# A Strassen–Winograd feed-forward block: seven products in one fixed PSUM tile, sums kept per product, four of them put back

## The chip, the cores and the metric

The kernel runs on one core of a Trainium2 chip. The metric is the device time of one execution in microseconds (us); lower is better. Engines: PE is the matrix engine (PEld its weight loads), DVE the vector engine, ACT the scalar engine, POOL the GpSimd engine, SP the engine that issues most DMAs. PSUM is the memory that PE writes; the other engines read it from there.

## The reference

One decoder layer for 544 tokens (512 of a prompt, 8 times 4 of samples): attention and gated delta rule, then cross attention, then a gated feed-forward block. The change touches only the last:

```python
    hf = rmsnorm(x, p['norm_ffn_g'])
    gate, up = jnp.split(hf @ p['w_gate_up'], 2, axis=-1)   # 2048 -> 2 x 5632
    x = x + (jax.nn.silu(gate) * up) @ p['w_down']          # 5632 -> 2048
```

All is float32.

## The kernel before, in words

Tokens lie side by side, T = 544 columns, in two halves of HT = 272; features lie on the 128 partitions. Every float32 operand is split exactly into two parts (a rounded high part by an ACT cast, the rest by a subtraction), and a product is three matmuls: high by high, high by low, low by high. Blocks of two by two are multiplied with Winograd's seven products P1 to P7 instead of eight.

**Gate and up** (`ffn`, the loop over `j`, 44 *rounds*). A round makes two output blocks of 128 features (one of gate, one of up) in `wino`: four *steps* `u`, each over two pairs of input blocks, each 42 matmuls of 272 columns (7 products x 2 pairs x 3). So a round has 168 matmuls, and a product is added up in PSUM over the four steps.

`left` makes a step's left operands: two DMAs of weights into `u`, four sums on POOL (L1613 to L1616), two casts on ACT (`wh`, 128x768 and 128x1024, L1620) and two subtractions on DVE (`wl`, L1621). `wh` and `wl` have two buffers each, so the casts of a step can begin when the step two before it has left PE. `combine` reads the seven products out of PSUM (ACT copies P1, L1661; DVE adds the others, L1673 to L1679), and `ffn` scales, applies silu and multiplies. Every second round POOL makes Winograd's four sums of the result (`sums`, L1572 to L1575) and ACT's queue stores them to `hT` in DRAM.

**Down** (the loop over `ci`, five *chunks* of 4, 4, 4, 4 and 6 pairs of hidden blocks). Each chunk has eight rounds `m` over the output blocks, of two steps (three in the last chunk). `fetch` loads a chunk's right operands from `hT` and splits them (L1590, L1591). After each round `combine` adds the two result blocks to `acc` (L1661 to L1671). The last chunk adds the residual `x` and stores.

**PSUM.** The products lie in two tiles of two banks out of a pool of two such tiles each (`c.mm`), and three single banks of four (`c.aux`).

**Order.** A scheduler of the language puts every engine's instructions in the order in which the program is written, with priorities; each engine then runs its own list strictly in order and waits on semaphores. The waits come from which tile an instruction reads or writes.

## Time and profile before

| | |
|---|---|
| median of 3 runs | 3056.04 us (3052.62 to 3064.1) |
| the profiled execution | span 3059.9 us; no other time of it is shown |
| granted PE clock, mean | 0.983 |
| PE, DVE, POOL, ACT busy | 95%, 70%, 55%, 45% of the span |
| gate and up | 1549.7 to 2491.9 us of the span |
| down | 2491.9 to 3059.9 us |
| DMA | 392.67 MB, mean 128 GB/s |

How to read it: times in the rows are microseconds, or nanoseconds for the mean of one instruction. In a timeline row the bracket at the end is the idle time of the engine just before, and the instruction that ended it. PEclk is the clock that PE was granted, as a part of full speed. Matmuls overlap: one shows about 0.29 us but the next starts 0.125 us later.

### The profile page before, as it was taken

The numbers are of one execution on the slowest core, as the hardware profiler recorded it, in microseconds if no ns is written. First come the engines' busy times: TensorE is split into PE (matmuls) and PEld (weight loads), VectorE is DVE, ScalarE is ACT, GpSimd is POOL, SyncE is SP. The second block draws the span as 40 slices with busy tenths as digits, with TensorE's granted clock in tenths as the row PEclk, the third lists the DMA queues.
The fourth block names the chain that finished last, engine by engine and source line by source line (L and its number), as shares of the span: only waits on it lengthen the run. The fifth ranks groups of instructions, "written<-read, shape, count | busy, mean of one in ns | idle before, by whom it ended". The sixth has DMA issues, their size and how long they took to land.

```text
span 3059.9 us, 58347 instructions
## 1 busy us (share of the span) xinstructions
PE 2900.2 (95%) x22118; PEld 2789.1 (91%) x22118; DVE 2134.3 (70%) x3339; ACT 1363.5 (45%) x2600; POOL 1671.8 (55%) x1784
## 2 busy tenths in 40 slices
PE   8999999999999999999799999999999989988898
PEld 7999998889899999999689999999999989988797
DVE  6776775655655655366687777777777888888865
ACT  5544453435645654245543343333333344334333
POOL 3211122312112100032378988898888977999997
PEclk9999999999999999999899999999999999999999
DMA  7323233544535765423434344333434354344343
GB/s 212 95 80 85 75 88 99 144 137 147 173 105 151 227 197 150 127 81 116 161 117 127 118 122 123 121 117 118 125 118 123 116 179 132 110 131 127 119 137 105
DMA packets 619505, 392.67 MB, mean 128 GB/s; under 512 B 36475, under 2 KB 572360, under 8 KB 619224
## 3 DMA queue, kind: packets, MB, share of 16 engines
q1 hardware_dynamic: 596904, 355.95, 39.6%
q10 hardware_dynamic: 22320, 32.99, 3.0%
q8 instruction: 174, 2.85, 0.4%
q14 instruction: 107, 0.88, 0.1%
HBM read 334.17 MB, written 54.68 MB: 127 GB/s over the span
## 4 chain that ended last, share of the span: by engine, by line
POOL 27%; PE 20%; DVE 8%; issue 4%; DMA 4%; ACT 2%; SPq 0%; POOLq 0%; ACTq 0%; DVEq 0%
PE mm L208 7%; POOL u L1615 6%; POOL u L1613 6%; POOL u L1614 5%; PE mm L1647 5%; POOL u L1616 5%; PE aux L1647 4%; DVE wl L1621 3%; DMA u<-in_w_gate_up 2%; DVE pr L1591 2%; PE aux L1342 2%; POOL acc L1670 1%; PE mm L1530 1%; POOL x L1572 1%; PE aux L960 1%
## 5 line engine op out<-in xcount | busy, mean ns | idle before, releaser
L1621 DVE TENSOR_TENSOR wl<-u,wh 128x768 fp32r<-128x768 f32 (+1 forms) x528 | 752.5, 1442 | 315.9 <-ACT wh L1620 213.6
L1647 PE MATMUL mm<-pr,wh 128*128 128x272 f32 x4224 | 830.6, 292 | 41.6 <-DVE acc L1663 25.3
L1620 ACT CAST wh<-u 128x768 fp32r<-128x768 f32 (+1 forms) x528 | 488.8, 943 | 826.5 <-PE aux L1647 295.4
L1647 PEld LDWEIGHTS mm<-pr,wh 128*128 128x128 f32 x4224 | 669.4, 191 | 50.5 <-DVE acc L1663 20.3
L1647 PE MATMUL aux<-pr,wh 128*128 128x272 f32 x3168 | 626.9, 292 | 17.7 <-DVE acc L1669 6.7
L1647 PE MATMUL mm<-pr,wl 128*128 128x272 f32 x2112 | 615.7, 292 | 22.5 <-DVE wl L1621 22.5
L208 PE MATMUL mm<-ah,wh 128*128 128x272 f32 (+1 forms) x2464 | 538.6, 298 | 5.7 <-ACT ah L321 4.6
L1647 PEld LDWEIGHTS aux<-pr,wh 128*128 128x128 f32 x3168 | 506.8, 192 | 21.7 <-DVE acc L1669 8.6
L208 PE MATMUL mm<-al,wh 128*128 128x272 f32 (+1 forms) x2464 | 524.3, 291 | 0.7 <-DVE al L239 0.7
L208 PE MATMUL mm<-ah,wl 128*128 128x272 f32 (+1 forms) x2464 | 515.6, 290 | 0.1
L1647 PE MATMUL aux<-pr,wl 128*128 128x272 f32 x1584 | 460.9, 291 | 2.0 <-DVE wl L1621 2.0
L1647 PEld LDWEIGHTS mm<-pr,wl 128*128 128x128 f32 x2112 | 403.3, 191 | 28.4 <-DVE wl L1621 28.4
L208 PEld LDWEIGHTS mm<-ah,wh 128*128 128x128 f32 (+1 forms) x2464 | 391.9, 189 | 28.8 <-issue 8.5
L197 DVE TENSOR_TENSOR wl<-wr,wh 128x512 fp32r<-128x512 f32 (+1 forms) x366 | 264.0, 725 | 195.9 <-ACT wh L196 186.7
L208 PEld LDWEIGHTS mm<-al,wh 128*128 128x128 f32 (+1 forms) x2464 | 389.6, 188 | 5.4 <-issue 2.0
L208 PEld LDWEIGHTS mm<-ah,wl 128*128 128x128 f32 (+1 forms) x2464 | 386.2, 188 | 2.5 <-DVE wl L197 0.5
L196 ACT CAST wh<-wr 128x512 fp32r<-128x512 f32 (+1 forms) x366 | 224.3, 615 | 336.6 <-PE mm L208 272.6
L1613 POOL TENSOR_TENSOR u<-u 128x256 f32<-128x256 f32 x264 | 277.3, 1050 | 140.8 <-DMA u<-in_w_gate_up 90.2
L1615 POOL TENSOR_TENSOR u<-u 128x256 f32<-128x256 f32 x264 | 323.2, 1224 | 0.0
L1616 POOL TENSOR_TENSOR u<-u 128x256 f32<-128x256 f32 x264 | 308.5, 1169 | 19.1
L1647 PEld LDWEIGHTS aux<-pr,wl 128*128 128x128 f32 x1584 | 303.7, 192 | 2.6 <-DVE wl L1621 2.4
L1614 POOL TENSOR_TENSOR u<-u 128x256 f32<-128x256 f32 x264 | 270.4, 1024 | 0.0
(518 smaller groups left out, 3809.1 us busy)
## 6 DMA issues: line engine op xcount, KB each, us to landing
u<-in_w_gate_up SPq DMA_DIRECT2D x352, 256.0 KB
wr<-in_w_in SPq DMA_DIRECT2D x108, 512.0 KB
u<-in_w_down SPq DMA_DIRECT2D x176, 256.0 KB
v<-hT SPq DMA_DIRECT2D x66, 272.0 KB
page<-in_cache_sb_k SPq DMA_DIRECT2D x128, 128.0 KB
page<-in_cache_sb_v SPq DMA_DIRECT2D x64, 256.0 KB
wr<-in_w_out SPq DMA_DIRECT2D x32, 512.0 KB
hT<-x ACTq DMA_DIRECT2D x44, 272.0 KB
```

The costliest lines, as they stand in the source:

```text
L196: nc.scalar.copy(hi[:, :m, :n], raw[:, k : k + m, :n])
L197: nc.vector.tensor_sub(lo[:, :m, :n], raw[:, k : k + m, :n], hi[:, :m, :n].bitcast(F32))
L208: c.nc.tensor.matmul(ps[:n, h, :HT], l[:, :n], r[:, h * HT : (h + 1) * HT], start=first and i == 0, stop=last and i == 2,)
L1342: nc.tensor.matmul(ps[:, :256], l, r, start=k == 0 and n == 0, stop=k == 7 and n == 2)
L1591: nc.vector.tensor_sub(lo[:, o : o + n * HT], x[:, : n * HT], hi[:, : n * HT].bitcast(F32))
L1613: nc.gpsimd.tensor_add(s1, a21, a22)
L1614: nc.gpsimd.tensor_sub(s3, a11, a21)
L1615: nc.gpsimd.tensor_sub(s2, s1, a11)
L1616: nc.gpsimd.tensor_sub(s4, a12, s2)
L1620: nc.scalar.copy(hi, u[:, o : o + n])
L1621: nc.vector.tensor_sub(lo, u[:, o : o + n], hi.bitcast(F32))
L1647: nc.tensor.matmul(ps, l[:, cols], r, start=u + i == 0 and j == 0, stop=u + i == n - 1 and j == 2)
```

## The change

What lies ahead of the feed-forward block is as it was. In it:

1. One PSUM tile `bank` of seven banks holds the seven products, in fixed places, for all rounds; `aux` has one bank left. Products are made in another order (P1, P7, P6, P2, P5, P4, P3).
2. `combine` is one ACT copy of P1 and five DVE operations (two of 544 columns), all on `bank`.
3. `left` puts the weights in `raw` and the sums in a tile of their own; three of the four sums go from POOL to DVE, with other formulas.
4. `hT` holds the split parts, seven tiles of 544 columns a pair. The split (ACT cast, POOL subtraction) is done once, in the gate-and-up loop, and seven stores a pair go out on ACT's queue. `fetch` is seven DMAs a pair on POOL's queue straight into the operand tiles.
5. In the down part, each of the eight rounds `m` keeps its seven product sums in SBUF (class `Sums`). P1, P6 and P7 are added to by DVE after each round; P2 to P5 are copied by ACT back into their banks ahead of the next chunk's round (`seed`), whose matmuls add to them, and are copied out by ACT after it. The residual is added in chunk 1. The combination is done once, in the last chunk (`finish`).

The core of the diff:

```diff
 def left(c, w, k, ca, cb):
-    u = c.wu.tile([P, 8, 2 * P], F32, tag="u", name="u", bufs=3)
+    a, b = (c.wu.tile([P, 4, 2 * P], F32, tag=x, name=x, bufs=n) for x, n in (("raw", 3), ("sum", 2)))
...
-    nc.gpsimd.tensor_add(s1, a21, a22)
-    nc.gpsimd.tensor_sub(s3, a11, a21)
-    nc.gpsimd.tensor_sub(s2, s1, a11)
-    nc.gpsimd.tensor_sub(s4, a12, s2)
+    nc.vector.tensor_sub(b[:, 2], a[:, 0], a[:, 2])
+    nc.vector.tensor_add(b[:, 1], b[:, 2], a[:, 1])
+    nc.gpsimd.tensor_add(b[:, 0], a[:, 0], a[:, 1])
+    nc.vector.tensor_sub(b[:, 3], a[:, 3], b[:, 1])
...
-    ma, mb = c.mm(), c.mm()
-    p4, p7, p3 = (c.aux()[:, :HT] for _ in range(3))
-    todo = ((p1, 1, 0), (p2, 2, 1), (p4, 0, 6), (p6, 4, 4), (p5, 3, 3), (p7, 5, 5), (p3, 6, 2))
+PRODUCTS = ((P1, 1, 0), (P7, 5, 5), (P6, 4, 4), (P2, 2, 1), (P5, 3, 3), (P4, 0, 6), (P3, 6, 2))
...
+                    nc.tensor.matmul(
+                        c.bank[:, p, :HT], l[:, cols], r,
+                        start=u + i == 0 and j == 0 and p not in seeded, stop=u + i == n - 1 and j == 2,
+                        skip_group_check=p in seeded,
+                    )
...
+def combine(c, y, z):
+    nc.scalar.copy(s1, bank[:, P1])
+    nc.vector.tensor_add(u2, s1, bank[:, P6])
+    nc.vector.tensor_add(y[:, :HT], s1, bank[:, P2])
+    nc.vector.tensor_add(halves(e), bc(u2.rearrange("p (o x) -> p o x", o=1), [P, 2, HT]), bank[:, P7 : P5 - 1 : -1])
+    nc.vector.tensor_add(halves(z), bc(u3.rearrange("p (o x) -> p o x", o=1), [P, 2, HT]), bank[:, P4 : P5 + 1])
+    nc.vector.tensor_add(y[:, HT:], u4, bank[:, P3])
...
+class Sums:
+    def seed(self):
+        for x, b, n in self.parts[3:1:-1]:
+            self.c.nc.scalar.copy(self.c.bank[:, b : b + n, :HT], x)
+    def keep(self, added=False):
+        for i, (x, b, n) in enumerate(self.parts):
+            if added and i < 2:
+                self.c.nc.vector.tensor_add(x, x, self.c.bank[:, b : b + n, :HT])
+            else:
+                self.c.nc.scalar.copy(x, self.c.bank[:, b : b + n, :HT])
...
+                nc.gpsimd.dma_start(t, src[:, i])
...
+            for i, x in enumerate((*v, *sums(c, *v, nc.gpsimd))):
+                hi, lo, n, _ = part_of(c, x, lambda: c.hp.tile([P, T], F32R, tag="st", name="hs", bufs=4), 2 if i else 1, nc.gpsimd)
+                for t in (hi, lo)[2 - n :]:
+                    nc.scalar.dma_start(hT[j // 2, :, len(tiles)], t[:, :].bitcast(F32))
...
+            wino(c, c.w_down, 2 * first[ci], m * P, (m + 1) * P, pairs, step, 0, SEEDED if ci else ())
+            acc[m // 2].keep(ci > 0)
+            if ci == 1:
+                acc[m // 2].residual(*x)
             if last:
+                acc[m // 2].finish()
...
+    c.bank = banks.tile([P, 7, 512], F32, name="bank")
+    c.aux = lambda: banks.tile([P, 512], F32, tag="aux", name="aux", bufs=1)
```

How the instructions stand now is shown at three places. In the rows, `waits PE_49` and the like name the engines whose semaphores an instruction waits on.

ACT at the end of a gate-and-up round (the twelfth), before: the copy of P1 out of PSUM is the row `COPY g<-mm`; the two casts ahead of it belong to the next round's first step, those behind it to its second and third.

```order
L1620 CAST wh<-u 128x768 [waits DMAHW5_49,DVE_49,DMAHW7_49,PE_49,Activation_49]
L1620 CAST wh<-u 128x1024 [waits DVE_49,PE_49,Pool_49]
L1661 COPY g<-mm 128x272 [waits PE_49]
L1620 CAST wh<-u 128x768 [waits DMAHW0_49,DMAHW1_49,DVE_49,PE_49]
L1620 CAST wh<-u 128x1024 [waits DVE_49,PE_49,Pool_49]
```

The same place after; `b` is the copy of P1, and the four casts are those of the next round's steps 0 and 1:

```order
L1624 CAST wh<-raw 128x768 [waits DMAHW0_49,DMAHW7_49,DVE_49,PE_49]
L1624 CAST wh<-sum 128x1024 [waits DVE_49,PE_49,Pool_49]
L1624 CAST wh<-raw 128x768 [waits DMAHW2_49,DMAHW3_49,DVE_49,PE_49]
L1624 CAST wh<-sum 128x1024 [waits DVE_49,PE_49,Pool_49]
L1668 COPY b<-bank 128x272 [waits PE_49]
L1749 ACTIVATE g<-g 128x544 [waits DVE_49]
L1594 CAST hs<-u 128x544 [waits DVE_49]
L1758 DMA hT<-hs 128x544 [waits Activation_49]
L1758 DMA hT<-hs 128x544 [waits Pool_49]
```

The copy of P1 moved from behind two casts of the next round to behind four, and its wait is now for the last matmul of the round, the last to write `bank`. Behind it, four split casts and seven stores take the place of three stores.

DVE at the same boundary, before; `b`, `g` and `u` are the combination's tiles:

```order
L1621 TENSOR_TENSOR wl<-u,wh 128x768 [waits DMAHW0_49,DMAHW1_49,PE_49,Activation_49]
L1673 TENSOR_TENSOR b<-g,mm 128x272 [waits PE_49]
L1674 TENSOR_TENSOR g<-g,mm 128x272 [waits DVE_49]
L1675 TENSOR_TENSOR g<-b,mm 128x272
L1676 TENSOR_TENSOR b<-b,aux 128x272 [waits PE_49]
L1679 TENSOR_TENSOR g<-g,aux 128x272 [waits DVE_49,PE_49]
L1677 TENSOR_TENSOR u<-b,mm 128x272 [waits DVE_49]
L1678 TENSOR_TENSOR u<-b,aux 128x272
```

And after:

```order
L1625 TENSOR_TENSOR wl<-raw,wh 128x768 [waits PE_49,Activation_49]
L1625 TENSOR_TENSOR wl<-sum,wh 128x1024 [waits PE_49,Activation_49]
L1669 TENSOR_TENSOR b<-b,bank 128x272 [waits Activation_49]
L1670 TENSOR_TENSOR g<-b,bank 128x272
L1671 TENSOR_TENSOR e<-b,bank 128x544 [waits DVE_49]
L1617 TENSOR_TENSOR sum<-raw 128x256 [waits DMAHW7_49,DMAHW6_49]
L1672 TENSOR_TENSOR u<-e,bank 128x544 [waits DVE_49]
L1673 TENSOR_TENSOR g<-e,bank 128x272
```

The `wl` of 1024 columns (of step 1) now stands ahead of the combination, and one weight sum (L1617) inside it.

PE at the start of a round, after (the first two rows are the last of the old round, P3):

```order
L1653 MATMUL bank<-pr,wh 128x272 x2
L1653 MATMUL bank<-pr,wl 128x272
L1653 MATMUL bank<-pr,wh 128x272 [waits DVE_49,Activation_49]
L1653 MATMUL bank<-pr,wh 128x272
L1653 MATMUL bank<-pr,wl 128x272
```

The round's first matmul (P1) waits there, in the program's semaphores, for the DVE row L1673 and the ACT row L1668 above; no later product's first matmul waits for a reader of its bank.

ACT at a round's end in the down part, before (chunk 1); `a` is P1's copy, `pr<-v` casts of fetched operands:

```order
L1590 CAST pr<-v 128x544 [waits DMAHW7_49]
L1590 CAST pr<-v 128x544 [waits DMAHW4_49]
L1620 CAST wh<-u 128x1024 [waits DVE_49,PE_49,Pool_49]
L1661 COPY a<-mm 128x272 [waits PE_49]
L1620 CAST wh<-u 128x768 [waits DMAHW6_49,DMAHW7_49,DVE_49,PE_49]
```

And after; `a_30334` and `a_30333` are the kept P4, P5 and P2, P3 of the round that ends, `a_30457` and `a_30458` those of the next round:

```order
L1624 CAST wh<-raw 128x768 [waits DMAHW6_49,DMAHW7_49,DVE_49,PE_49]
L1624 CAST wh<-sum 128x1024 [waits DVE_49,PE_49,Pool_49]
L1699 COPY a_30334<-bank 128x544 [waits DVE_49,PE_49,Activation_49]
L1699 COPY a_30333<-bank 128x544
L1691 COPY bank<-a_30457 128x2x272 [waits Activation_49]
L1691 COPY bank<-a_30458 128x2x272 [waits Activation_49]
L1624 CAST wh<-raw 128x768 [waits DMAHW1_49,DMAHW0_49,PE_49]
```

One copy of 272 columns became two copies out and two copies back, of 544 columns each.

## The prediction

> **What bounds the kernel now.** First the page's busy times and its slices, then stretches of the feed-forward part, then PE's timeline at the ends of rounds.

> ```profile
> PE 2900.2 (95%) x22118; PEld 2789.1 (91%) x22118; DVE 2134.3 (70%) x3339; ACT 1363.5 (45%) x2600; POOL 1671.8 (55%) x1784
> ...
> PEclk9999999999999999999899999999999999999999
> ```

> PE is busy 95% of the span at nearly full clock: the end is set by how rarely PE stands still. The change leaves all before 1549.7 us as it was, so I read the two parts behind it (columns: window, its length, then busy time of PE, PEld, DVE, ACT and POOL, granted clock, DMA share, GB/s).

> ```profile
> 1549.70:2491.90 942.20, 916.63 (x7229) 908.72 (x7229) 729.89 (x794) 366.96 (x448) 838.53 (x777) 1.00 0.41 124
> 1718.00:1761.30 43.30, 42.50 (x336) 42.18 (x336) 33.52 (x37) 16.76 (x21) 39.20 (x37) 1.00 0.39 120
> 2491.90:3059.90 568.00, 505.86 (x3773) 493.20 (x3773) 447.87 (x544) 226.24 (x349) 504.78 (x424) 0.94 0.43 126
> ```

> Gate and up: two rounds (336 matmuls) in 43.30 us, PE busy 42.50 of them. Down: 568 us, of which PE stands still 62.1, at a clock of 0.94. At the end of a gate-and-up round PE's timeline reads:

> ```profile
> 1704.07 0.41 PE L1647 MATMUL aux<-pr,wh 128*128 128x272 f32 x2
> 1704.32 0.28 PE L1647 MATMUL aux<-pr,wl 128*128 128x272 f32 x1
> 1704.44 0.41 PE L1647 MATMUL mm<-pr,wh 128*128 128x272 f32 x2
> ...
> 1718.35 0.40 PE L1647 MATMUL mm<-pr,wl 128*128 128x272 f32 x1 [0.76 <-DVE wl L1621]
> ...
> 1761.64 0.39 PE L1647 MATMUL mm<-pr,wl 128*128 128x272 f32 x1 [0.79 <-DVE wl L1621]
> ```

> At 1704.44 the next round's first product (mm) follows the last product of the old one (aux) with no idle bracket: three matmuls from 1704.07 to 1704.44 are 0.37 us, so 0.125 us each, and a round of 168 is 21.0 us. The only regular wait is one of 0.8 us in two rounds, for a `wl`. From 1718.35 to 1761.64 the pair of rounds takes 43.29 us, 1.29 more than 42.0.

> Why the boundary is free now stands in the timelines of ACT and DVE:

> ```profile
> 1700.89 0.39 ACT L1661 COPY g<-mm 128x272 f32<-128x272 f32 x1 [0.55 <-PE mm L1647]
> 1704.56 1.05 ACT L1620 CAST wh<-u 128x1024 fp32r<-128x1024 f32 x1 [2.22 <-DVE g L1675]
> ...
> 1703.25 0.43 DVE L1673 TENSOR_TENSOR b<-g,mm 128x272 f32<-128x272 f32 x1
> 1703.72 0.44 DVE L1674 TENSOR_TENSOR g<-g,mm 128x272 f32<-128x272 f32 x1
> 1704.07 0.43 DVE L1675 TENSOR_TENSOR g<-b,mm 128x272 f32<-128x272 f32 x1
> ```

> P1 is copied out at 1700.89, 3.5 us before the round ends, and three more products are read before 1704.44; the next round writes other PSUM tiles anyhow.

> **The change, part by part.** *A. The boundary of gate and up.* With one tile `bank`, the copy of P1 waits for the round's last matmul, and the next round's first matmul waits for the last DVE read (L1673) of the combination. Nothing of PE's work can lie beside this. Behind the round's end come, in series: ACT's cast of 1024 columns for the next round's step 1 (its buffer is that of step 3, which only then is free), then DVE's `wl` of it, which stands ahead of the combination, then the combination. ACT's copy lies beside `wl`. The prices:

> ```profile
> L1620 ACT CAST wh<-u 128x1024 fp32r<-128x1024 f32 x259 | 272.0, 1050 | 657.4 <-PE aux L1647 192.8 <-POOL u L1616 186.6 <-POOL x L1575 142.9
> L1621 DVE TENSOR_TENSOR wl<-u,wh 128x1024 fp32r<-128x1024 f32 x259 | 408.2, 1576 | 254.2 <-ACT wh L1620 152.4 <-POOL u L1614 96.4 <-PE aux L1647 4.2
> ...
> 2618.98 1.23 DVE L1621 TENSOR_TENSOR wl<-u,wh 128x1024 fp32r<-128x1024 f32 x1 [0.47 <-ACT wh L1620]
> ...
> L1671 DVE TENSOR_TENSOR acc<-acc,b 128x544 f32<-128x544 f32 x1 | 0.7, 722 | 0.0
> L1661 ACT COPY a<-mm 128x272 f32<-128x272 f32 x32 | 12.3, 386 | 4.9 <-PE mm L1647 4.8
> ```

> Cast 1.05; `wl` 1.23 (an undisturbed one; its mean is 1.58); the combination by the starts above, 0.35 for each of the three 272-column operations (0.43 the last), 0.65 for each of the two of 544 (0.72 by the row, less the overlap of 0.08), and some 0.35 for the weight sum of 256 columns among them: 2.8; three changes of engine, an estimate of 0.2 each from the 0.12 between PE's 1704.44 and ACT's cast at 1704.56: 0.6. Together 5.7 us of idle PE; 5.3 (no weight sum) and 6.2 (the mean `wl`) are the ends.

> *B. The clock behind a gap.* The rows of before show what follows such gaps:

> ```profile
> 2491.89 0.79 PE L1647 MATMUL mm<-pr,wh 128*128 128x272 f32 x2 [6.54 <-DVE g L1674]
> 2492.48 0.43 PE L1647 MATMUL mm<-pr,wl 128*128 128x272 f32 x1
> ...
> 2496.15 0.42 PE L1647 MATMUL mm<-pr,wh 128*128 128x272 f32 x2
> ...
> 2506.91 0.52 PE L1647 MATMUL mm<-pr,wh 128*128 128x272 f32 x2 [1.60 <-DVE acc L1674]
> 2507.27 0.29 PE L1647 MATMUL mm<-pr,wl 128*128 128x272 f32 x1
> ...
> 2610.88 0.52 PE L1647 MATMUL mm<-pr,wh 128*128 128x272 f32 x2 [2.46 <-DVE acc L1663]
> ...
> 2612.00 0.43 PE L1647 MATMUL mm<-pr,wl 128*128 128x272 f32 x1
> ...
> 2615.39 0.29 PE L1647 MATMUL mm<-pr,wl 128*128 128x272 f32 x1
> ...
> 2491.90:2495.90 4.00, 4.00 (x18) 4.00 (x19) 4.00 (x8) 1.43 (x3) 3.84 (x6) 0.50 0.63 186
> ```

> After 6.54 us idle, matmuls come 0.22 us apart, not 0.125, and the granted clock of that window is 0.50. The 19 matmuls to 2496.15 took 4.26 us, not 2.4: 1.9 lost. After 2.46 us idle the same happens a little later: the 15 from 2612.00 to 2615.39 took 3.39 us, not 1.9: 1.5 lost. After 1.60 us there is none. So I take 1.7 us a boundary here; 0 and 2.2 are the ends.

> [...]

> Sum of A and B: 43 x (5.7 + 1.7) = 318 us (the 44th is in the down part). What before lost, 1.29 in two rounds, goes: -28.

> *C. POOL's subtractions in ACT's way.* In every second round ACT now issues seven stores that wait for POOL's subtractions of low parts, with casts behind them. Nearest rows: POOL's operations of 544 and 272 columns, and ACT's wait of before for `sums`.

> ```profile
> L1671 POOL TENSOR_TENSOR acc<-acc,b 128x544 f32<-128x544 f32 x31 | 53.5, 1724 | 3.0 <-DVE b L1668 3.0
> L1575 POOL TENSOR_TENSOR x<-u,x 128x272 f32<-128x272 f32 x22 | 17.0, 774 | 1.7
> ...
> ACT wh L1620 <- POOL x L1575: 142.9, 19, 8.9
> ```

> ACT waited 7.5 us for POOL there already, with 0.8 us of it reaching PE. Four sums (3.5) and four subtractions (6 to 7), with two weight sums of about 1 between, are some 13 us behind the combination, while step 2's operands are due 10.5 us after the round's start: 1.3 us late, 22 times: +29. Ends 0 and 4 x 22 = 88. The sums of weights that leave POOL (three per step, 1 us each) and join DVE (three of about 0.4) are hidden: DVE's step becomes 1.2 + 0.95 + 1.23 = 3.4 of 5.25 us; without that cover a step would be 0.4 longer per operation.

> *D. Down.* Chunk 0: a boundary is the cast 1.05, then ACT's copies out of 544, 272, 544 and 544 columns, and by this row 0.64 for 544:

> ```profile
> L1590 ACT CAST pr<-v 128x544 fp32r<-128x544 f32 x66 | 41.2, 643 | 29.1 <-DMA v<-hT 28.7 <-PE mm L1647 0.4
> L1776 ACT ACTIVATE y<-aux,unscale 128x128 f32<-128x128 f32 x64 | 18.0, 367 | 12.9 <-PE aux L960 12.9
> ...
> PE mm L1647 <- DVE acc L1663: 25.3, 12, 7.4
> ...
> 2990.46 0.54 PE L1647 MATMUL aux<-pr,wh 128*128 128x272 f32 x2 [1.01 <-DVE acc L1669]
> ...
> 3030.92 0.52 PE L1647 MATMUL aux<-pr,wh 128*128 128x272 f32 x2 [1.01 <-DVE acc L1669]
> ```

> 1.05 + 3 x 0.64 + 0.39 + 0.3 = 3.6, and 1.6 for the clock: 8 x 5.2 = 42. Chunks 1 to 3: cast, two copies out, two back (a copy into PSUM is in no row; it is taken as one out of it, ends half and double), 1.05 + 4 x 0.64 + 0.3 = 3.9; DVE's additions to P1, P6 and P7 lie beside: 24 x (3.9 + 1.6) = 132, ends 24 x 3 and 24 x 7. Chunk 4: two rounds now take 40.46 us (2990.46 to 3030.92), 20.2 a round against 126 x 0.125 = 15.75 of matmuls. After, the four `y` activations (1.5) stand in ACT ahead of the copies, and the transposes of `y` stay (some 1.5): 15.75 + 1.5 + 1.5 + 3.9 + 1.6 = 24.2: 8 x 4.0 = 32. What goes: waits for L1663 (25.3 us in 12) and a few us of half clock at the ends of chunks, where fetched parts were split by ACT and DVE and are not now: -29; ends 0 and -62, all of PE's idle time there. The fetch has no cast to wait for, but POOL's queue issues it, and weight sums stand behind DMAs that wait for a free tile; before the first round of down 28 of them stand ahead of L1619. I take that as hidden by the two steps of operands made ahead, and 10 us for each of five chunks if not.

> Sum of C and D: 29 + 42 + 132 + 32 - 29 = 206. In all 3059.9 + 318 - 28 + 206 = 3556, say **3555 us**. The profiled execution lies 0.1% above the median of the three runs, which I neglect. One per cent of this kernel is 31 us; 0.5% is about what a measurement can tell from no change.

> **Rivals.** *The clock stays up.* If gaps at a steady beat don't lower the clock, 43 x 1.7 + 40 x 1.6 = 137 us go: 3420. For it: 1.60 us idle did nothing. Against it: the rows at 2491.89 and 2610.88.

> *More waits.* C at its end (+60) and the fetch on POOL's queue not hidden (+50), with `wl` at its mean (0.35 x 43 = 15) and seeds somewhat dearer (+15): 3690. For it: POOL was busy 838.53 of 942.20 us in gate and up, and ACT's queue is strictly in order. Against: POOL gives three of its four weight sums away.

> *Banks come free one by one.* If the first matmul had only to wait for P1's reader, the boundary would be cast 1.05, copy 0.39 and 0.3 of changes, 1.75 us, which is below the gap that lowers the clock: 43 x 1.75 - 28 + 29 = 76, and some 65 in down: 3200. For it: each product has its own bank. Against: the order of instructions shows the wait on L1673. [...]

> *Faster.* If the boundary is covered: PE's first matmul comes within 1 us of the round's end because ACT and DVE do the copies before the next casts. The gains are then the 28 of gate and up, the 62 of PE's idle time in down and some 10 of half clock: 2960. It decides below 100 us in 83 boundaries, 1.2 us each; the cast alone, 1.05, and the copy, 0.39, are more.

> **How the numbers follow.** Forecast 0.62 (its own range 3470 to 3630, from the ends of A and of the seeds); clock stays up or falls seldom 0.14; more waits 0.14; single banks 0.06; faster 0.04. From 3400 to 3700 the range takes in the first three and leaves out the last two with the outer parts of the others. Faster by over 0.5%: 0.04; within 0.5%, a boundary of just 1.2 us: 0.01; slower: 0.95.

> **What would show it.** In the new trace: per gate-and-up round one idle bracket of 5.3 to 6.2 us on PE, released by DVE L1673; 168 matmuls then, the first 15 to 19 at 0.22 us; rounds of 28 us. In down, 3.5 to 4 us behind ACT L1691. PE busy falls near 85%. Wrong would be: no idle bracket at the round's start, a release by ACT L1668, spacing of 0.125 right behind the gap, or step 2 waiting many us for `wh`.

## The result, and the profile after

The changed kernel takes 3528.02 us (median of 4 runs, 3524.49 to 3530.4) against 3057.98 us: 1.153 times the kernel before, with a 95% interval of 1.151 to 1.155. The profiled execution has a span of 3525.6 us, 465.7 more than that of before. The forecast was 3555 us, with 3400 to 3700 as its range.

The page after, busy times and the granted clock in 40 slices:

```profile
PE 3042.4 (86%) x22118; PEld 2923.5 (83%) x22118; DVE 2190.4 (62%) x3785; ACT 1442.0 (41%) x2720; POOL 846.1 (24%) x1180
...
PEclk9999999999999999989888888888888898888888
```

PE has as many matmuls as before and is busy 86% of a longer span; POOL's busy time is halved, and the time did not gain by it. From the 18th slice on the clock shows 8 nearly everywhere. What PE waited for in the feed-forward part (columns: total us, times, longest):

```profile
PE bank L1653 <- DVE g L1673: 219.4, 43, 5.3
PE bank L1653 <- ACT bank L1691: 114.2, 26, 4.9
PE bank L1653 <- ACT a L1699: 21.5, 7, 4.2
PE aux L960 <- DVE a L1713: 18.7, 8, 4.0
PE bank L1653 <- DVE wl L1625: 14.8, 22, 1.0
```

43 waits of 5.1 us for the last reader of the bank in gate and up, 26 of 4.4 us for the copies back in down. By stretches (window, length, busy time of PE, PEld, DVE, ACT, POOL, granted clock, DMA share, GB/s), first before, then after; each begins where gate and up or down begins:

```profile
1549.70:2485.35 935.65, 916.62 (x7228) 908.67 (x7228) 723.34 (x785) 362.05 (x441) 834.88 (x774) 1.00 0.41 123
2485.35:3059.90 574.55, 505.88 (x3773) 493.24 (x3773) 454.42 (x553) 231.15 (x357) 508.43 (x427) 0.94 0.43 128
```

```profile
1549.70:2796.60 1246.90, 1012.31 (x7234) 998.61 (x7233) 824.38 (x1205) 402.00 (x516) 337.74 (x362) 0.89 0.35 110
2796.60:3525.60 729.00, 550.27 (x3777) 536.79 (x3776) 408.31 (x561) 270.24 (x404) 191.02 (x250) 0.87 0.44 129
2018.35:2076.34 57.99, 47.14 (x336) 46.54 (x337) 38.45 (x57) 18.68 (x24) 15.33 (x16) 0.88 0.34 107
```

Gate and up lost 311.3 us, down 154.5: that is all of it. Two rounds take 57.99 us, where they took 43.3.

One boundary in the timelines of ACT, DVE and PE:

```profile
2099.34 0.83 ACT L1624 CAST wh<-raw 128x768 fp32r<-128x768 f32 x1 [3.42 <-PE bank L1653]
2100.14 1.04 ACT L1624 CAST wh<-sum 128x1024 fp32r<-128x1024 f32 x1
...
2101.22 1.23 DVE L1625 TENSOR_TENSOR wl<-sum,wh 128x1024 fp32r<-128x1024 f32 x1
...
2102.36 0.43 DVE L1669 TENSOR_TENSOR b<-b,bank 128x272 f32<-128x272 f32 x1
...
2104.80 0.42 DVE L1673 TENSOR_TENSOR g<-e,bank 128x272 f32<-128x272 f32 x1
...
2105.37 0.79 PE L1653 MATMUL bank<-pr,wh 128*128 128x272 f32 x2 [5.18 <-DVE g L1673]
```

The chain stands as forecast: PE stops at 2100.19 (the bracket says 5.18 us idle), the cast runs from 2100.14, `wl` from 2101.22, the five reads from 2102.36 to 2105.22, and PE goes on 0.15 us later.

### The profile page after: what moved, and what is told of

It is laid out like the page before. It is cut to its first block, busy times and chain, and to the rows that moved or that the text cites. A ratio compares the mean times of both kernels' runs of the same rounds, so it can differ in the third digit from the quotient of the medians.

```text
span 3525.6 us, 58389 instructions
## 1 busy us (share of the span) xinstructions
PE 3042.4 (86%) x22118; PEld 2923.5 (83%) x22118; DVE 2190.4 (62%) x3785; ACT 1442.0 (41%) x2720; POOL 846.1 (24%) x1180
## 4 chain that ended last, share of the span: by engine, by line
PE 47%; DVE 9%; ACT 6%; POOL 3%; issue 2%; DMA 2%; ACTq 0%; DVEq 0%; POOLq 0%; SPq 0%
PE bank L1653 37%; PE mm L208 6%; DVE wl L1625 3%; ACT wh L1624 3%; POOL hs L1595 1%; PE aux L1342 1%; ACT a L1699 1%; PE mm L1530 1%; ACT bank L1691 1%; DVE e L1671 1%; DMA pr<-hT 1%; DVE u L1672 1%; PE aux L960 1%; DVE a L1697 1%; DVE sum L1617 1%
## 5 line engine op out<-in xcount | busy, mean ns | idle before, releaser
L1653 PE MATMUL bank<-pr,wh 128*128 128x272 f32 x7392 | 1549.4, 309 | 364.4 <-DVE g L1673 219.4
L1653 PEld LDWEIGHTS bank<-pr,wh 128*128 128x128 f32 x7392 | 1286.0, 209 | 382.2 <-issue 231.3
L1653 PE MATMUL bank<-pr,wl 128*128 128x272 f32 x3696 | 1135.3, 307 | 20.6 <-DVE wl L1625 20.5
L1653 PEld LDWEIGHTS bank<-pr,wl 128*128 128x128 f32 x3696 | 768.2, 208 | 26.7 <-DVE wl L1625 26.7
L1625 DVE TENSOR_TENSOR wl<-raw,wh 128x768 fp32r<-128x768 f32 x264 | 267.3, 1013 | 646.4 <-PE bank L1653 443.5
L1624 ACT CAST wh<-raw 128x768 fp32r<-128x768 f32 x264 | 220.1, 834 | 855.5 <-PE bank L1653 838.0
L1619 POOL TENSOR_TENSOR sum<-raw 128x256 f32<-128x256 f32 x264 | 254.8, 966 | 1121.4 <-DVE wl L1625 1077.4
L1625 DVE TENSOR_TENSOR wl<-sum,wh 128x1024 fp32r<-128x1024 f32 x264 | 335.6, 1271 | 29.6 <-ACT wh L1624 21.7
L1624 ACT CAST wh<-sum 128x1024 fp32r<-128x1024 f32 x264 | 277.1, 1049 | 46.4 <-PE bank L1653 24.1
L1618 DVE TENSOR_TENSOR sum<-sum,raw 128x256 f32<-128x256 f32 x264 | 181.5, 694 | 5.7
L1617 DVE TENSOR_TENSOR sum<-raw 128x256 f32<-128x256 f32 x264 | 131.8, 505 | 40.4 <-DMA raw<-in_w_down 34.2
L1620 DVE TENSOR_TENSOR sum<-raw,sum 128x256 f32<-128x256 f32 x264 | 114.8, 442 | 7.1
## 6 DMA issues: line engine op xcount, KB each, us to landing
hT<-hs ACTq DMA_DIRECT2D x154, 272.0 KB
pr<-hT POOLq DMA_DIRECT2D x154, 272.0 KB, 6.2
```

Of the source, the lines that this page charges most:

```text
L1617: nc.vector.tensor_sub(b[:, 2], a[:, 0], a[:, 2])
L1618: nc.vector.tensor_add(b[:, 1], b[:, 2], a[:, 1])
L1619: nc.gpsimd.tensor_add(b[:, 0], a[:, 0], a[:, 1])
L1620: nc.vector.tensor_sub(b[:, 3], a[:, 3], b[:, 1])
L1624: nc.scalar.copy(hi, x)
L1625: nc.vector.tensor_sub(lo, x, hi[:, :, :].bitcast(F32))
```

## The experiments

In every one the ratios are set against the kernel before, run beside it on the same chip (3057 to 3061 us). The changed kernel's 3528 us is from the measurement above and was not taken again beside the experiments.

**1. Seven tiles in place of one.** The products, and every read of them, in tiles of one bank each:

```diff
-    c.bank = banks.tile([P, 7, 512], F32, name="bank")
+    c.bank = [banks.tile([P, 512], F32, name=f"bank{i}") for i in range(7)]
```

> The changed kernel with seven tiles of one bank each in place of the one tile of seven banks; every read of PSUM is then of 272 columns, and a product's first matmul has to wait only for the readers of its own bank. Theory (the time went into boundaries at which PE waits for the whole tile to be read): the idle time of 5.1 us and the 2.2 us of low clock at each of 43 gate-and-up boundaries go (-314), and most of the 4.55 us (24 times) and 2.9 us (8 times) in the down part with their low clock (-170): 3040 us, at most 3150. Rival (the time went into the fetch, the stores or the weight sums on DVE): within 50 us of 3528.

3076.46 us, 1.0053 times the kernel before (1.0033 to 1.0073). All but 16 of the 470 us are gone with an edit that makes more instructions (3905 on DVE, not 3785) and takes no work away. That the loss lay in waiting for the tile as a whole is thereby shown. What PE waited for now:

```profile
PE bank L1653 <- DVE wl L1625: 53.4, 51, 5.4
PE bank L1653 <- ACT wh L1624: 10.3, 23, 1.4
PE bank L1653 <- DMA pr<-hT: 7.8, 8, 3.3
```

These are operands. Waits for a reader of a bank, or for a copy back, are left with some 8 us in all, where they were 355. A boundary of gate and up now reads:

```profile
2031.77 0.42 DVE L1672 TENSOR_TENSOR u<-e,bank 128x272 f32<-128x272 f32 x1
2031.83 0.29 PE L1653 MATMUL bank<-pr,wl 128*128 128x272 f32 x1
2031.95 0.42 PE L1653 MATMUL bank<-pr,wh 128*128 128x272 f32 x2
2032.15 0.44 DVE L1673 TENSOR_TENSOR g<-e,bank 128x272 f32<-128x272 f32 x1
2032.20 0.29 PE L1653 MATMUL bank<-pr,wl 128*128 128x272 f32 x1
2032.33 0.41 PE L1653 MATMUL bank<-pr,wh 128*128 128x272 f32 x2
```

DVE's last read (L1673) runs beside the next round's matmuls, and PE has no idle bracket. The 16 us that are left are a sum of two larger amounts: two gate-and-up rounds take 46.2 us here and took 43.3 before, while the down part is some 40 us shorter than before.

**2. The combination first.** An edge in the order puts ACT's copy of P1 and DVE's reads ahead of the cast and the `wl` of 1024 columns:

```diff
+            for ins in behind if n == 4 else ():
+                s.enter_context(c.tc.issue_after(getattr(ins, "ins", ins)))
             nc.scalar.copy(hi, x)
             nc.vector.tensor_sub(lo, x, hi[:, :, :].bitcast(F32))
```

> The changed kernel with one edge in the order: in gate and up, ACT's cast and DVE's subtraction for the next round's step 1 (1024 columns) stand behind the reading of the bank, not ahead of it. Theory: PE's gap falls from 5.1 us to a copy, five reads and three changes of engine, 3.0 to 3.1 us, 43 times 2.1 = -90 us, to 3438; what the low clock costs then may be anything from 0 to 2.2 us per boundary, so 3350 to 3450. Rival (the cast and the subtraction lie beside the reading, and something else sets the gap): gap as before, 3528.

3479.05 us: 49 less than the changed kernel, not the 78 that were the least expected. The boundary now:

```profile
2108.23 0.84 ACT L1627 CAST wh<-raw 128x768 fp32r<-128x768 f32 x1 [3.47 <-PE bank L1656]
2109.06 0.39 ACT L1671 COPY b<-bank 128x272 f32<-128x272 f32 x1
2109.10 0.96 DVE L1628 TENSOR_TENSOR wl<-raw,wh 128x768 fp32r<-128x768 f32 x1 [1.28 <-ACT wh L1627]
...
2109.98 0.43 DVE L1672 TENSOR_TENSOR b<-b,bank 128x272 f32<-128x272 f32 x1
...
2112.63 0.79 PE L1656 MATMUL bank<-pr,wh 128*128 128x272 f32 x2 [3.60 <-DVE g L1676]
```

The gap fell from 5.1 to 3.6 us, not to 3.05: the subtraction of 768 columns, still ahead on DVE, holds the first read until 2109.98. The two links did lie in series. The clock still fell, at 42 of the 43 boundaries, and some of the gain went to new waits for `wl` (27.6 us in 34 waits, 14.8 in 22 before).

**3. PE kept busy in the gap.** 24 matmuls whose result nobody reads, for each of 42 boundaries:

```diff
+            ps = c.aux()
+            for i in range(24):
+                nc.tensor.matmul(ps[:, :HT], pairs[0][0][0][:, :P], pairs[0][0][0], start=True, stop=True)
```

> The changed kernel with 24 idle matmuls (on average) into the spare bank at each gate-and-up boundary, whose result nobody reads; they take about 3 of the 5.1 us for which PE waits. Theory (behind a gap PE runs at a lower clock for some 15 to 25 matmuls, 2.2 us a boundary): these spells go, 42 times 2.2 = -90 us, 3430 to 3450, with the same wait for L1673 less the filling. Rival (the slow matmuls are slow for another reason, such as ACT and DVE reading PSUM at the same time): 3528, or more by what the filling delays.

3483.16 us, only 45 less. The trace tells why: nothing held the filling matmuls back, and they had gone into the first 25 boundaries, nearly always 40 or 41 in each, with the last 11 of them at the 26th. So the one trace holds both cases; two rounds with filling and two without:

```profile
2083.63:2137.67 54.04, 53.34 (x417) 52.46 (x417) 38.95 (x57) 18.70 (x25) 15.20 (x16) 1.00 0.37 116
2377.14:2434.76 57.62, 46.60 (x336) 45.94 (x337) 38.45 (x57) 18.68 (x24) 15.42 (x16) 0.91 0.35 108
```

With the gap filled the clock is 1.00 and the pair 3.6 us shorter (4 us against the changed kernel's pairs), while ACT and DVE read PSUM as before: that rules the rival out. Tied to the last matmul of each round:

> The changed kernel with 24 idle matmuls into the spare bank behind each of 42 gate-and-up rounds, tied to the round's last matmul (in the first such run they had all moved into the first 24 boundaries; two rounds took 54.3 us there and 58.0 us without them). Theory (the low clock behind a gap costs 1.9 us a boundary): two rounds take 54.3 us throughout, 42 times 1.87 = -79 us: 3440 to 3465 us. Rival (the gain of the first run came from something else at those boundaries): 3480 or more.

3460.58 us (3455.3 to 3465.87), within what was expected: 67 us for 42 boundaries, 1.6 us each. Not all of it is the clock: the waits for `wl` fell as well, from 14.8 to 4.0 us. And not all of the low clock went: 2.05 to 2.2 us of idle time were left at each boundary, and behind 21 of the 43 the clock still fell.

**4. No sums put back.** DVE adds all seven products to the kept sums:

```diff
-            if added and i < 2:
+            if added:
...
-                acc[m // 2].seed()
```

> The changed kernel without putting sums back: in chunks 1 to 4 all seven sums are added to by DVE after each round (operations of 544, 272, 544 and 544 columns), and every chunk's products start anew. Theory (a boundary costs the serial reading of the one tile; two copies back are two more links): PE's gap in chunks 1 to 3 falls from 4.55 us to 3.3 to 3.5 us, 24 times 1.1 = -27, and some in chunk 4: 3490 to 3505 us. Rival (putting the four sums back saves time against adding on DVE): 3528 or more.

3493.72 us, 34 less than the changed kernel. PE's gap in chunks 1 to 3 is 3.37 us (PE waits for DVE's additions to `a`, L1697), not 4.55. While one tile is read in series, the two copies back are two more links; here they cost, not save.

**5. The rest of the change alone.** PSUM tiles, combination and sums as in the kernel before, all else as changed:

```diff
-    c.bank = banks.tile([P, 7, 512], F32, name="bank")
+    c.pmm = ctx.enter_context(tc.tile_pool(name="pmm", bufs=2, space=PSUM))
+    c.pax = ctx.enter_context(tc.tile_pool(name="pax", bufs=4, space=PSUM))
```

> The PSUM tiles, the combination and the sums in the down part are those of the kernel before; the rest of the change stays: split parts in DRAM, fetched on POOL's queue without a cast, seven stores a pair, three weight sums on DVE. Theory (all that is lost is lost at the one tile): no slower than before, and faster by part of the 62 us for which PE stands still in the down part: 3000 to 3050 us. Rival (these other parts cost too): 3100 or more.

3155.97 us, 1.0313 times (1.0296 to 1.0331): my theory was wrong here. The rest is not free but costs 95 us once PSUM does not hide it. Two runs split that. With the three weight sums back on POOL as well:

```diff
-    nc.vector.tensor_sub(b[:, 2], a[:, 0], a[:, 2])
+    nc.gpsimd.tensor_sub(b[:, 2], a[:, 0], a[:, 2])
...
```

> The kernel with the PSUM tiles of before and the rest of the change (3156 us), with the three sums of weights back on POOL. Theory for its 95 us over the kernel before (PE waited 88 us in 42 waits for the DVE reading of the bank, which stood behind sums of weights and a subtraction): 3060 to 3085 us. Rival (the seven stores on ACT's queue or the splitting on POOL cost them): 3130 or more.

3203.82 us, 48 more: the theory was wrong, and with the splitting on POOL the sums on DVE are a help. With them on DVE, but whole blocks stored and fetched as before:

> The PSUM tiles, the combination and the sums of the kernel before, and its storing and fetching of whole blocks; of the change only the three weight sums on DVE, their formulas and tiles are left. Theory (the 95 us of the run with old PSUM tiles come from splitting and storing the parts in gate and up): 3040 to 3075 us. Rival (they come from the weight sums on DVE ahead of its reading of the banks): 3100 or more.

3076.86 us, 2 us over the range: 79 of the 95 us come with splitting and storing the parts, and they lie in gate and up, where two rounds took 48.2 us with it and 44.4 without. ACT waited for POOL's subtractions there (121.5 us in 42 waits for the next split, in the trace of the first of these runs). The last 20 remain with the sums on DVE (PE waited 43.4 us in 43 waits for DVE's L1681). The two parts do not simply add: without the splitting the sums on DVE cost 20 us, and beside it they save 48, because POOL would otherwise have both to do.

**6. What is left of the loss.** On the seven tiles, the stores of parts from POOL's queue:

```diff
-                    nc.scalar.dma_start(hT[j // 2, :, len(tiles)], t[:, :].bitcast(F32))
+                    nc.gpsimd.dma_start(hT[j // 2, :, len(tiles)], t[:, :].bitcast(F32))
```

> Seven tiles of one bank each, as before, and besides the seven stores of split parts per pair are issued by POOL's queue, not ACT's. In the run with seven tiles PE still waited 0.92, 0.41 and 1.09 us in every second gate-and-up round, and two rounds took 46.2 us. Theory (ACT's queue stands still at stores that wait for POOL's subtractions, and its casts of weights come late): these waits and the slow matmuls behind them go, 22 times 3 to 4 us: 2990 to 3020 us, under the kernel before. Rival (POOL is late whichever queue stores, or issuing costs POOL what ACT gains): 3060 or more.

3056.6 us, 0.9995 times the kernel before (0.9986 to 1.0004): 20 gained, not 60. Now DVE is taken up nearly all the time, working or held up; four rounds (columns as above), and two rows of the timelines of DVE and POOL:

```profile
1947.25:2037.21 89.96, 86.57 (x672) 84.68 (x672) 88.43 (x121) 37.12 (x48) 41.33 (x46) 1.00 0.45 138
```

```profile
1944.08 1.98 DVE L1620 TENSOR_TENSOR sum<-raw,sum 128x256 f32<-128x256 f32 x1
...
1944.39 1.37 POOL L1595 TENSOR_TENSOR hs<-x,hs 128x544 fp32r<-128x544 f32 x1
```

DVE is busy 88.43 of 89.96 us, and an operation that takes 0.42 us in the mean in the changed kernel (0.77 here) takes 1.98 beside POOL's subtraction: it ends 0.3 us after POOL does. What holds DVE up, and why not POOL, these two rows do not show: by them DVE had begun 0.31 us before POOL.

Whole blocks on the seven tiles:

> Seven tiles of one bank each, and the storing and fetching of the hidden blocks as in the kernel before: whole blocks, four stores a pair, split into parts by ACT and DVE in the down part (the tile of weight sums has one buffer, not two, to make room). Theory (with the tile out of the way, what is left of the loss in gate and up is ACT and DVE standing behind POOL's splitting): two gate-and-up rounds fall from 46.2 us (45.0 with POOL's stores) to 43 or less, the down part stays 30 to 45 us under that of before: 3010 to 3040 us. Rival (what is left is the three weight sums on DVE): 3056 or more.

3125.15 us. This tells nothing of the theory on gate and up: to make room, the weight sums had one buffer, and ACT's casts waited for DVE's sums (332.5 us in 110 waits from 1700 to 2400 us; 10.3 us in 3 waits for L1618 in nearly all of gate and up on the seven tiles of experiment 1). What it shows of the down part is said at the end of this section.

Last, the low parts subtracted on DVE, which then needs POOL less:

```diff
-                hi, lo, n, _ = part_of(c, x, lambda: ..., 2 if i else 1, nc.gpsimd)
+                hi, lo, n, _ = part_of(c, x, lambda: ..., 2 if i else 1, nc.vector)
```

> Seven tiles of one bank each (3076 us), and the low parts that are stored are subtracted on DVE, not POOL; ACT's queue still stores. Theory (what is left of the loss in gate and up is ACT's queue waiting for POOL's subtractions of 1.4 to 2.3 us each, and DVE's sums, 0.42 us alone and 0.7 to 0.8 beside POOL, slowed by them): ACT waits for DVE's 0.7 us instead, two gate-and-up rounds fall from 46.2 to 43 or 44 us: 3010 to 3040 us. Rival (DVE has no time left for them: it was busy 88.4 of 90 us in the run with POOL's stores): 3060 or more.

3016.44 us, 0.9863 times (0.9848 to 0.9878), within what was expected: two gate-and-up rounds take 43.1 us, and 60 of the 3076 us of experiment 1 are gone.

> As the run with low parts on DVE, and the stores issued by POOL's queue. Theory: neither ACT's casts nor DVE stand behind POOL; 3000 to 3035 us, and no more than the run with ACT's stores. Rival (POOL's issuing waits for DVE and holds up its weight sum, and with it the casts): more than the run with ACT's stores, 3056 or more.

3010.37 us (3010.09 to 3015.65), 0.9843 times the kernel before (0.9829 to 0.9856): 49 us faster than it, and 518 faster than the changed kernel. The same 600 us of gate and up, in the kernel before and in this one:

```profile
1800.00:2400.00 600.00, 588.55 (x4657) 584.13 (x4657) 460.59 (x501) 231.35 (x279) 538.80 (x501) 1.00 0.40 121
```

```profile
1800.00:2400.00 600.00, 594.42 (x4681) 589.53 (x4680) 576.20 (x894) 257.75 (x334) 234.25 (x263) 1.00 0.48 144
2478.39:3013.90 535.51, 498.66 (x3794) 488.18 (x3794) 406.22 (x602) 283.47 (x556) 192.21 (x259) 0.95 0.61 178
```

Gate and up is 0.5% faster there, some 5 us. The rest comes from down: from the last gate-and-up matmul that the trace has, 535.51 us, where the kernel before has 574.55. Is it the banks and sums, or the fetch that needs no cast? The down part of the two runs that fetch whole blocks and cast them, first with the old PSUM tiles and sums, then with the seven tiles and `Sums`:

```profile
2507.88:3072.90 565.02, 502.03 (x3768) 488.27 (x3768) 533.88 (x808) 227.00 (x351) 205.99 (x168) 0.96 0.43 128
2579.28:3119.00 539.72, 500.36 (x3797) 484.36 (x3797) 453.87 (x683) 321.30 (x633) 124.19 (x116) 0.98 0.47 139
```

With the same fetch (with fewer buffers in the second) it is 25 us shorter: fixed banks and kept sums pay, once each bank is a tile of its own. Which of the two pays, and whether putting sums back does, was not tried on the seven tiles.

## Why the prediction was right

**A, the boundary of gate and up: right.** 5.7 us forecast, with 5.3 as the lower end; 5.05 and 5.18 in turn. The changes of engine took 0.14 and 0.15 us, not 0.2, one had no length at all (the cast begins as the last matmul ends), and the mean fell 0.6 short: 25 us of the sum.

**B, the clock: right, with another size.** 1.7 us forecast; by the spacing of the matmuls the boundaries lost 1.9 and 2.6 us in turn, so 2.25: 23 us more. A and B together are 43 x 7.35 = 316 us, against 318; that the two errors cancel is luck. What B took for the cause, the length of the gap, is not all of it (see the last section), but the clock fell behind every gap of 5 us: at all 43 boundaries.

**The gain of 28 and C's loss of 29: neither came.** PE still waits 0.6 to 0.8 us for a `wl` in every second round. ACT did wait for POOL's splitting (111.3 us in 42 waits), yet PE waited for ACT's casts only once in gate and up and the down part together (1.7 us): the gap of 5 us at each boundary gave ACT the time back. The cover was the loss itself: with the boundary mended, C's cost appeared (experiments 5 and 6). I named its place and queue rightly, and put its price at 29 us, 88 at most, where the run with the old PSUM tiles showed some 79. That the two terms which did not come cancel in the sum is luck too.

**D, down: 177 forecast, 154.5 measured.** Three terms were off in size. The timelines of ACT, DVE and PE at a boundary of chunk 0 and one of chunk 1:

```profile
2876.11 1.04 ACT L1624 CAST wh<-sum 128x1024 fp32r<-128x1024 f32 x1
...
2877.06 1.92 ACT L1699 COPY a<-bank 128x544 f32<-128x544 f32 x4
...
2879.03 0.52 PE L1653 MATMUL bank<-pr,wh 128*128 128x272 f32 x2 [2.88 <-ACT a L1699]
2879.38 0.29 PE L1653 MATMUL bank<-pr,wl 128*128 128x272 f32 x1
...
3036.87 1.06 DVE L1697 TENSOR_TENSOR a<-a,bank 128x544 f32<-128x544 f32 x2
...
3038.04 1.13 ACT L1699 COPY a<-bank 128x544 f32<-128x544 f32 x2 [1.07 <-DVE a L1697]
3039.20 1.26 ACT L1691 COPY bank<-a 128x544 f32<-128x544 f32 x2
3040.52 0.52 PE L1653 MATMUL bank<-pr,wh 128*128 128x272 f32 x2 [4.55 <-ACT bank L1691]
...
3041.29 0.43 PE L1653 MATMUL bank<-pr,wl 128*128 128x272 f32 x1
...
3044.65 0.29 PE L1653 MATMUL bank<-pr,wl 128*128 128x272 f32 x1
```

In chunk 0 four copies follow each other in 1.92 us, not 2.3: a gap of 2.88, not 3.6. And in five of its eight boundaries the clock did not fall behind it, which I had counted at 1.6 us each: 26 us for the chunk, not 42. In chunks 1 to 3 the gap is 4.55 us, not 3.9. I had put DVE's additions to P1, P6 and P7 beside ACT's copies; ACT waits for them (1.07 us), so they are a link too. A copy into PSUM, of which no row spoke before, took 0.63 us, as taken. With what the ends of chunks cost before, these 24 rounds took 108 us more; forecast were 132 - 29 = 103. Chunk 4 took 23 us more, not 32. (The three make 157; the wait before the first round of down was 3 us shorter than before.)

**The rivals.** *The clock stays up* is ruled out: it fell at all 43 boundaries of gate and up. *Single banks* is what happened once each bank was a tile: the rows of experiment 1 show DVE reading one bank while PE writes another, and it was the program's wait that did not allow it. Its price, 3200, was set 124 us too high, for I left the boundary in series there. *Faster* needed a boundary under 1.2 us; it came with the seven tiles and DVE's splitting, at 3010 (2960 was said).

## What to carry to other kernels

Look in the order of instructions for what the first matmul of a round waits for. If it is the last reader of everything, the reading is in series with the matmuls, whatever the banks allow; give each bank a tile of its own before counting instructions. A cost that a trace does not show may only be covered by a larger one: after mending the boundary, the cost that I had put at 29 us stood up at some 79 with the old PSUM tiles, and the two runs that took its subtractions off POOL gained 60 and 66 us on the seven. And where DVE is nearly full, work given to POOL is not off its path: in experiment 6 a DVE sum of 0.42 us took 1.98 beside a POOL subtraction, and in experiment 5 one form of POOL's subtractions took 2.34 us in the mean with the weight sums on DVE, and 1.36 with them on POOL.

## What the runs showed of the hardware

```profile
2873.92:2877.33 3.41, 2.23 (x18) 2.01 (x17) 2.12 (x4) 2.02 (x3) 0.31 (x1) 1.00 0.33 97
2877.33:2880.75 3.42, 1.72 (x13) 1.72 (x14) 2.76 (x4) 1.65 (x4) 0.97 (x1) 1.00 0.53 153
2880.75:2884.16 3.41, 3.41 (x30) 3.41 (x29) 0.00 (x0) 0.46 (x1) 0.00 (x0) 1.00 0.00 0
3037.77:3041.18 3.41, 0.66 (x5) 0.66 (x6) 3.34 (x4) 2.36 (x4) 2.45 (x2) 1.00 0.53 154
3041.18:3044.59 3.41, 3.41 (x17) 3.41 (x17) 1.69 (x2) 0.00 (x0) 3.40 (x5) 0.50 0.34 85
3044.59:3048.01 3.42, 3.42 (x29) 3.42 (x28) 0.41 (x1) 1.28 (x2) 1.69 (x4) 1.00 1.05 288
```

In chunk 0 the gap of 2.88 us is divided, 1.18 us in one window and 1.70 in the next, and the clock stays. In chunk 1 one window holds 2.75 us of idle time, and the next runs at half clock, although PE is busy from end to end of it (17 matmuls, against 29 in the window behind it). I added up PE's idle time in every window of the feed-forward part, in all 14 traces. After a window at full clock with 1.9 us or more of it the next was at half clock, 433 times of 433; with less than 1.4 us, 4 times of 5494; between, 37 times of 184. After a window at half clock 0.8 us was enough to stay there, 255 times of 255; with less than 0.6 us the clock came back 460 times of 465. In the traces of the kernel before and the changed one alone the counts are, in the same order, 89 of 89, 0 of 747, 2 of 24, 67 of 67 and 90 of 90.

So a gap of 2.88 us left the clock up where it was divided over two windows, as at those five boundaries of chunk 0, whose rounds of 13.64 us are four windows long and so stay in step. Of a gap of 4.55 or 5.1 us some window holds 2.27 us or more, over those 1.9, and the clock fell at all 24 and all 43 of them in the changed kernel; of those of 2.05 to 2.2 us in experiment 3, 21 of 43 lowered the clock. And two short waits in one window did what a long one does: in the kernel before, waits of 1.03 and 1.01 us in the window from 2987.43 were enough, and the next, from 2990.84, ran at 0.50.
